# Gates of a decoder layer: six pairs of column chunks with seven products for eight, and another use of the weight buffers

## The chip, the core and the metric

The kernel runs on one core of a Trainium2 chip. The metric is the device time of one execution in microseconds (us). A core has TensorE (PE, matmuls; PEld is its weight load), VectorE (DVE), ScalarE (ACT), GpSimd (POOL) and SyncE (SP, which issues most of the DMAs). Each engine works off its own instructions in a fixed order; semaphores make one wait for another. Operands lie in SBUF, sums of matmuls in eight PSUM banks.

## What is computed

One layer on 256 tokens of width 2048, in float32. Its parts, cut from the reference:

```python
h = layer_norm(ALPHA * h + 0.5 * swiglu(h, w_ffn1_up, w_ffn1_down), ln1_g, ln1_b)
mix = token_mix(h, mem, w_in, b_gate, ...)
h = layer_norm(ALPHA * h + mix, ln2_g, ln2_b)
h = layer_norm(ALPHA * h + 0.5 * swiglu(h, w_ffn2_up, w_ffn2_down), ln3_g, ln3_b)

def token_mix(...):
    z = h @ w_in
    q, k, v, qi, ki, wi, u, qm, gl = split(z)
    a = dsa_attention(q, k, v, qi, ki, wi)      # 8 heads of 128, the 64 best keys of an indexer
    p = multiscale_pool(u, w_pool, pool_scale)
    m = memory_attention(qm, mem, w_mem_kv)     # 4 heads
    gates = sigmoid(gl + b_gate).reshape(B, S, 3, D)
    y = gates[0] * (a @ w_br_att) + gates[1] * (p @ w_br_pool) + gates[2] * (m @ w_br_mem)
    return y @ w_out
```

The gates are the part that the change touches: a product of the 256 x 2048 activations with 2048 x 6144 weights, 3 branches of 4 column chunks of 512.

## The kernel before

**Precision.** Every fp32 operand is split into a high and a low part (fp32r): ACT casts the high part (L105), DVE subtracts for the low one (L106). A product is three matmuls, high x high, high x low, low x high. Weights come by SP in halves of 128x1024 (two of the 128-row blocks of a group of 512 rows, `load_half`), into nine `raw` buffers; `halves` splits one into small buffers `wh` and `wl`, four of each, or, if `paged`, into two pages of the common pool `pg`.

**Work on PE.** `gemm` makes one 512-wide column chunk for both token halves (tt0, tt1, one PSUM bank each): 2 x 16 x 3 = 96 matmuls (L161) for a depth of 2048. With `head` or `tail` it holds some groups of weights back and runs tt0 over them, then tt1, so that one half begins or ends sooner; the line with `paged=` says which held halves lie in pages. `pair` makes two column chunks at once and saves one of eight quarter products in the first group of rows (seven products for eight, by sums of weights and sums of activations, `forms`): 186 matmuls (L231) for 192. Its sums of weights are DVE's (L256, L267, L272, L273). It consists of a front (one, two, five, six, seven), a middle and a back of whole quarters. `stream` weaves the front of the next pair with the back of the last, which is held in `self.back`; `flush` ends it. FFN1, FFN2 and their down products use pairs (20 for up, and some of the down products); the gates before do not.

**Delayed work.** `later` queues generators (the transposes of a chunk, `place`; the heads of an attention, `attend_heads`, six stages for four heads), and `tick` advances the first of them by one stage. A `gemm` ticks once per group of four blocks, `stream` once behind each middle step from the third on. One stage of `attend_heads` is the scores of one head (L445 on PE; L463, L465, L438, L440, L441 on DVE, the exponential L439 on ACT), the transposes of the head before (L477 and the split into `pt`) and the weighted sum of the one before that (L445 into `tr`, `weigh`). The order on each engine is set once, when the kernel is built, by the order of the program and by the scheduler's idea of what is ready.

**Order around the gates.** `attend(0)` makes q, k and v of heads 0 to 3 and queues their attention; gate(0) follows (three gemms, one for each branch), then `attend(1)`, gate(1), the rest of the queue, branch(0), gate(2), branch(1), gate(3), branch(2), branch(3). A gate adds its bias on DVE (L829) and takes tanh on ACT (L830). `branch` multiplies (L871) and adds the branches (L876, L877). Then come w_out with norm2 (`project_norm`), whose second token half is normalised inside FFN2's first gemm (`between=rest`), and FFN2 with norm3. In `Norm`, L554 (L552 for the first sum) adds the product to the residual, L556 and L605 take the statistics, L595 and L597 apply them in four pieces for each token half, and the last L597s write what goes out.

Of the kernel before, what the change touches and what calls it, by code (L numbers as in the profile page):

```python
# [17 lines left out]
P = 128  # L18
# [6 lines left out]
ND = D_MODEL // 512  # L25
# [9 lines left out]
TAKEN = -3e38  # L35
W_CHUNKS = dict(q=(0, 1), k=(2, 3), v=(4, 5), qi=(6, 7), u=(8,), qm=(9,))
GL0 = 10
PAGES = dict(pg=22, gt=6)
TMPS = 8
HIDDEN = ((0, 4), (4, 8), (8, NFF))  # L40

# [1 line left out]
class Layer:  # L43
# [19 lines left out]
    def hold(self, page):  # L63

        self.mark = self.nc.gpsimd.tensor_copy(self.tile("held", [P, 1], F32, 2), page.bitcast(F32)[:, :1])
# [18 lines left out]
        return self.sb.tile(shape, dt, name=f"{tag}_{self.n}", tag=tag, bufs=bufs)  # L84

    def page(self, dt=F32, tag="pg"):
        return self.tile(tag, [P, 1024], dt, PAGES[tag])

    def pages(self, n, dt=F32R, tags=()):
# [57 lines left out]
    def gemm(self, act, w, groups, head=0, tail=0, before=None, cut=None, between=None):  # L147

        nc = self.nc
        accs = [self.acc(), self.acc()]
        kts = 4 * groups
        self.products = []

        def step(tt, kt, wh, wl):
            ah, al = act(kt, tt)
            for i, (a, b) in enumerate(((ah, wh), (ah, wl), (al, wh))):  # L160
                self.products.append(nc.tensor.matmul(accs[tt], lhsT=a, rhs=b, start=kt == 0 and i == 0,  # L161
                                                      stop=kt == kts - 1 and i == 2))

        held = []
        for g in range(groups):
            if before is not None:
                before(g)
            ws = self.load_w(w[g], paged=g < head - 2 or groups - tail <= g < groups - 2,
                             cut=cut if g == 0 else None)
            parts = [(4 * g + kk, ws[kk // 2][0][:, kk % 2, :], ws[kk // 2][1][:, kk % 2, :]) for kk in range(4)]  # L170
            held += parts
            if g < head - 1 or groups > g + 1 > groups - tail:
                continue
            if g == head - 1 or g >= groups - tail:
                order = [(tt, part) for tt in range(2) for part in held]
            else:
                order = [(tt, part) for part in held for tt in range(2)]
            for i, (tt, part) in enumerate(order):
                if between is not None and g == head - 1 and i == len(held):
                    between()  # L180
                step(tt, *part)
            held = []
            self.tick()
        return accs
# [107 lines left out]
    def stream(self, parts):  # L292

        front, middle, back = parts
        behind = self.back
        for i in range(max(len(front), len(behind))):
            for step in behind[i:i + 1] + front[i:i + 1]:
                step()
        self.back = back
        for i, step in enumerate(middle):  # L300
            step()
            if i > 1:
                self.tick()
# [20 lines left out]
    @staticmethod  # L324
    def part(page, tt):
        return page.rearrange("p (k t) -> p k t", k=4)[:, :, tt * P:(tt + 1) * P]
# [86 lines left out]
    def project_norm(self, act, w, groups, resid, g, b, finish):  # L413

        norm = Norm(self, resid, g, b)
        norm.load()
        norm.load_scales()
        norm.add(act, w, groups, True, True, None, 4)
        return norm.finish(finish, defer=True)

    def norm_to_feature(self, dram):
# [196 lines left out]
def layer_kernel(ctx: ExitStack, tc: tile.TileContext, x, xT, memT, up1, down1, w_in, w_kw, b_gate, w_kv, w_pool,  # L618
                 pool_scale, br_att, br_pool, br_mem, w_out, up2, down2, ln, consts, band_c, out):
    nc = tc.nc  # L620
    L = Layer(ctx, tc)
# [70 lines left out]
    hh, hl = L.out_pages  # L692
    act = L.act_pages(hh, hl)
# [22 lines left out]
    for kt in range(KD):  # L716
        c = slice((kt % 8) * P, (kt % 8) * P + P)
# [14 lines left out]
    for i in range(2):  # L732
        r, c = slice(64 * i, 64 * i + 64), slice(256 * i, 256 * i + 256)
# [83 lines left out]

    gates = {}

    def gate(c):  # L820
        for br in range(3):
            n = br * ND + c
            accs = L.gemm(act, w_in[GL0 + n], 4)
            bg = L.tmp()
            nc.gpsimd.dma_start(bg, bass.AP(tensor=b_gate.tensor, offset=b_gate.offset + 512 * n, ap=[[0, P], [1, 512]]))
            gt = gates[br, c] = L.page(tag="gt")
            for tt in range(2):
                s = gt[:, 512 * tt:512 * tt + 512]
                nc.vector.tensor_add(s, accs[tt], bg)  # L829
                nc.scalar.activation(s, s, AF.Tanh, scale=0.5)  # L830

    ah, al = L.pages(2), L.pages(2)

# [13 lines left out]
    def attend(hf):  # L847
        q = feature_chunk(proj("q", hf), SCALE)
        k = feature_chunk(proj("k", hf))
        v = token_chunk(proj("v", hf))  # L850
        L.drain()
        if hf == 0:
            choose()
        L.later(L.attend_heads(4, *q, *k, *v, ah[hf], al[hf], 4 * hf, True, (dist, msel)))

    attend(0)
    gate(0)
    attend(1)
    gate(1)
    L.drain()  # L860
    yh, yl = [], []

    def branch(c):
        acts = ((L.act_pages(ah, al), br_att, 2), (L.act_pages([ph], [pl]), br_pool, 1),
                (L.act_pages([mh], [ml]), br_mem, 1))
        for br, (a, w, groups) in enumerate(acts):
            accs = L.gemm(a, w[c], groups)
            gt = gates[br, c]
            for tt in range(2):
                s = gt[:, 512 * tt:512 * tt + 512]  # L870
                nc.vector.scalar_tensor_tensor(s, s, 1.0, accs[tt], op0=ALU.add, op1=ALU.mult)  # L871
        yh.append(L.page(F32R))
        yl.append(L.page(F32R))
        for tt in range(2):
            g = [gates[br, c][:, 512 * tt:512 * tt + 512] for br in range(3)]
            nc.vector.tensor_add(g[0], g[0], g[1])  # L876
            nc.vector.tensor_add(g[0], g[0], g[2])  # L877

        def place():
            for tt in range(2):  # L880
                L.to_feature(gates[0, c][:, 512 * tt:512 * tt + 512], yh[c], yl[c], tt, 0.5)
            yield

        L.later(place())

    branch(0)
    gate(2)
    branch(1)
    gate(3)
    branch(2)  # L890
    branch(3)

# [78 lines left out]
```

## Time and profile before

| | |
|---|---|
| median of 3 runs | 2205.24 us (2204.08 to 2206.10) |
| profiled execution | 2204.89 us, its span 2203.0 us |
| granted TensorE clock, mean | 0.997 |
| busy: PE, DVE, ACT, POOL | 99%, 73%, 50%, 2% |
| chain that ended last | PE 97%, DVE 1%, DMA 1% |
| mean DMA rate | 201 GB/s |

Busy shares are means over the whole span; the rows by stage further on say which engine waits where. FFN1 fills the span up to about 700 us, the mixing block from there to about 1475 us, FFN2 the rest. A row `L106 DVE ... wl<-raw,wh` is a weight half's low part. The time in square brackets in a row of a timeline is the idle time of the engine before it, and what ended it.

### The profile page before, as it was taken

The page shows a single profiled execution, that of the slowest core. Times are in us where ns is not written, and L with a number is a line of the kernel's source. Part 1 is how long each engine was busy: PE and PEld are TensorE (multiplying, and loading weights), DVE is VectorE, ACT ScalarE, POOL GpSimd, SP SyncE. Part 2 cuts the span into 40 slices and gives each one's busy share as a digit, 9 for nine tenths or more (in the row PEclk, how much of TensorE's full clock was granted, in tenths as well). Part 3 has the DMA queues.
Part 4 walks back from the last instruction along what each step waited for, and adds up shares of the span by engine and source line. Part 5 has one row for each costly group of instructions (what it writes and reads, how often), then busy time and mean ns, then how long its engine had stood idle before and what let it go on. Part 6 is the DMA issues. An engine that isn't in the chain of part 4 may idle for free.

```text
span 2203.0 us, 26381 instructions
## 1 busy us (share of the span) xinstructions
PE 2181.2 (99%) x9886; PEld 1805.4 (82%) x9886; DVE 1607.1 (73%) x1819; ACT 1099.9 (50%) x1257; POOL 54.4 (2%) x98
## 2 busy tenths in 40 slices
PE   9999999999999999999999999999999999999997
PEld 7888888888888888888888888878888888888886
DVE  6878777887787858574566556677788677877786
ACT  5654555554554545544444444434555555545552
POOL 0000000000000100000000000000000000000000
PEclk9999999999999999999999999999999999999999
DMA  7575665565667645556655556754656655655762
GB/s 278 208 241 173 213 209 180 193 208 201 218 207 235 237 157 194 182 177 198 203 177 191 194 190 219 245 197 157 234 197 208 209 180 198 204 196 186 246 207 87
DMA packets 123136, 442.47 MB, mean 201 GB/s; under 512 B 14256, under 2 KB 14768, under 8 KB 123008
## 3 DMA queue, kind: packets, MB, share of 16 engines
q1 hardware_dynamic: 115632, 416.34, 55.1%
q0 software_dynamic: 6800, 22.36, 3.3%
q10 hardware_dynamic: 576, 2.10, 0.3%
q8 instruction: 77, 1.26, 0.2%
q14 instruction: 51, 0.42, 0.1%
HBM read 434.44 MB, written 6.29 MB: 200 GB/s over the span
## 4 chain that ended last, share of the span: by engine, by line
PE 97%; DVE 1%; DMA 1%; ACT 0%; issue 0%; POOLq 0%; POOL 0%; DVEq 0%; SPq 0%; ACTq 0%
PE acc L231 56%; PE acc L161 38%; PE tr L321 2%; PE tr L445 1%; DMA raw<-in_up 1%; DVE wl L106 0%; ACT wh L105 0%; PE tr L477 0%; DVE pg L106 0%; DVE gt L595 0%; DVE tmp L385 0%; DVE raw L267 0%; DVE gt L597 0%; PE tr L801 0%; DVE stats L556 0%
## 5 line engine op out<-in xcount | busy, mean ns | idle before, releaser
L106 DVE TENSOR_TENSOR wl<-raw,wh 128x1024 fp32r<-128x1024 f32 (+1 forms) x866 | 1054.2, 1220 | 532.7 <-ACT wh L105 522.7
L105 ACT CAST wh<-raw 128x1024 fp32r<-128x1024 f32 (+1 forms) x866 | 910.4, 1052 | 963.0 <-PE acc L231 444.4
L231 PE MATMUL acc<-wh,pg 128*128 128x512 f32 x3656 | 1137.6, 390 | 0.0
L231 PEld LDWEIGHTS acc<-wh,pg 128*128 128x128 f32 x3656 | 686.0, 188 | 142.4 <-DVE pg L106 0.6
L161 PE MATMUL acc<-wh,pg 128*128 128x512 f32 x2416 | 755.5, 390 | 1.2 <-ACT wh L105 1.0
L231 PE MATMUL acc<-wl,pg 128*128 128x512 f32 x1828 | 711.5, 389 | 0.3
L161 PEld LDWEIGHTS acc<-wh,pg 128*128 128x128 f32 x2416 | 453.8, 188 | 96.0 <-ACT wh L105 2.9
L161 PE MATMUL acc<-wl,pg 128*128 128x512 f32 x1208 | 470.7, 390 | 0.8 <-DVE wl L106 0.8
L231 PEld LDWEIGHTS acc<-wl,pg 128*128 128x128 f32 x1828 | 343.3, 188 | 71.1 <-DVE wl L106 1.1
L161 PEld LDWEIGHTS acc<-wl,pg 128*128 128x128 f32 x1208 | 227.0, 188 | 47.5 <-DVE wl L106 1.7
L362 ACT COPY tmp<-acc 128x512 f32<-128x512 f32 x80 | 47.1, 589 | 27.1 <-PE acc L231 27.1
L106 DVE TENSOR_TENSOR pg<-tr,pg 128x512 fp32r<-128x512 f32 x82 | 54.5, 683 | 0.4 <-ACT pg L105 0.3
L569 DVE TENSOR_TENSOR gt<-gt,acc 128x512 f32<-128x512 f32 x64 | 43.2, 681 | 6.0 <-PE acc L231 6.0
L105 ACT CAST pg<-tr 128x512 fp32r<-128x512 f32 x82 | 45.7, 589 | 0.0
L272 DVE TENSOR_TENSOR raw<-raw,raw 128x1024 f32<-128x1024 f32 x30 | 36.7, 1224 | 1.0
L267 DVE TENSOR_TENSOR raw<-raw,raw 128x1024 f32<-128x1024 f32 x30 | 36.7, 1224 | 1.0
L273 DVE TENSOR_TENSOR raw<-raw,raw 128x1024 f32<-128x1024 f32 x30 | 36.7, 1224 | 0.8
L256 DVE TENSOR_TENSOR raw<-raw,raw 128x1024 f32<-128x1024 f32 x30 | 36.7, 1224 | 0.8
L161 PE MATMUL acc<-pg,pg 128*128 128x512 f32 x120 | 30.7, 410 | 4.6 <-DVE pg L106 2.4
L321 PEld LDWEIGHTS tr<-ident,tmp 128*128 128x128 f32 x240 | 29.1, 140 | 6.5
L321 PE MATMUL tr<-ident,tmp 128*128 128x128 f32 x240 | 34.3, 272 | 0.0
L161 PEld LDWEIGHTS acc<-pg,pg 128*128 128x128 f32 x120 | 23.2, 197 | 11.0 <-DVE pg L106 3.7
(124 smaller groups left out, 672.6 us busy)
## 6 DMA issues: line engine op xcount, KB each, us to landing
raw<-in_up SPq DMA_DIRECT2D x350, 512.0 KB, 4.7
raw<-in_down SPq DMA_DIRECT2D x176, 512.0 KB, 4.5
raw<-in_w_in SPq DMA_DIRECT2D x176, 512.0 KB, 3.9
raw<-in_w_out SPq DMA_DIRECT2D x32, 512.0 KB, 4.7
raw<-in_w_kv SPq DMA_DIRECT2D x16, 512.0 KB, 4.9
raw<-in_br_att SPq DMA_DIRECT2D x16, 512.0 KB, 4.0
h_d<-gt POOLq DMA_DIRECT2D x16, 256.0 KB, 5.1
raw<-in_br_pool SPq DMA_DIRECT2D x8, 512.0 KB, 3.8
```

The source lines that it names most:

```text
L105: self.nc.scalar.copy(h, src)
L106: self.nc.vector.tensor_sub(l, src, h.bitcast(F32))
L161: self.products.append(nc.tensor.matmul(accs[tt], lhsT=a, rhs=b, start=kt == 0 and i == 0, stop=kt == kts - 1 and i == 2))
L231: nc.tensor.matmul(banks[bank], lhsT=a, rhs=b[:, k, :], start=fresh and k == 0 and i == 0, stop=(close is not None or left[bank] == 0) and ...
L256: nc.vector.tensor_add(raw["00"], raw["00"], raw["01"])
L267: nc.vector.tensor_add(raw["00"], raw["00"], raw["11"])
L272: nc.vector.tensor_add(raw["00"], raw["00"], raw["10"])
L273: nc.vector.tensor_add(raw["01"], raw["01"], raw["11"])
L321: self.nc.tensor.transpose(t[:, i * P:(i + 1) * P], src[:, i * P:(i + 1) * P], self.ident)
L362: nc.scalar.copy(s[name], bank)
L445: self.nc.tensor.matmul(out, lhsT=a, rhs=b, start=start and i == 0, stop=stop and i == 2)
L569: (nc.vector.tensor_sub if name in ("16", "167") else nc.vector.tensor_add)(zz, zz, bank)
```

## The change

The gates become six pairs: `gate(br, c, forms)` makes the chunks c and c+1 of one branch. gate(0,0) stands behind `attend(0)` and is flushed; gate(1,0) and gate(2,0) behind `attend(1)`; gate(0..2, 2) behind branch(0) and branch(1). The forms of the activations are made once, behind `attend(0)`. The sums of a pair (`take`) go to DVE, seven or eight of 128x512 for a pair. `stream` ticks behind each front step too. The two sets of pages (22 and 6) become one of 28. Of held groups the first two now use the small buffers and the later ones pages, and w_out's tail is 3 groups, no longer 4.

```diff
-PAGES = dict(pg=22, gt=6)
+PAGES = dict(pg=28)
...
     def page(self, dt=F32, tag="pg"):
+        tag = "pg"
         return self.tile(tag, [P, 1024], dt, PAGES[tag])
...
-            ws = self.load_w(w[g], paged=g < head - 2 or groups - tail <= g < groups - 2,
+            ws = self.load_w(w[g], paged=2 <= g < head or g >= groups - tail + 2 > 2,
                              cut=cut if g == 0 else None)
...
             for step in behind[i:i + 1] + front[i:i + 1]:
                 step()
+            self.tick()
...
-        norm.add(act, w, groups, True, True, None, 4)
+        norm.add(act, w, groups, True, True, None, 3)
...
-    def gate(c):
-        for br in range(3):
-            n = br * ND + c
-            accs = L.gemm(act, w_in[GL0 + n], 4)
-            bg = L.tmp()
-            nc.gpsimd.dma_start(bg, bass.AP(tensor=b_gate.tensor, offset=b_gate.offset + 512 * n, ap=[[0, P], [1, 512]]))
-            gt = gates[br, c] = L.page(tag="gt")
-            for tt in range(2):
-                s = gt[:, 512 * tt:512 * tt + 512]
-                nc.vector.tensor_add(s, accs[tt], bg)
+    def gate(br, c, forms):
+
+        bg = []
+        for n in (br * ND + c, br * ND + c + 1):
+            bg.append(L.tmp())
+            nc.gpsimd.dma_start(bg[-1], bass.AP(tensor=b_gate.tensor, offset=b_gate.offset + 512 * n,
+                                                ap=[[0, P], [1, 512]]))
+        gt = [L.page(tag="gt") for _ in range(2)]
+        for i in range(2):
+            gates[br, c + i] = gt[i]
+
+        def take(name, bank):
+            to = {"1": "00", "5": "01", "16": "01", "167": "11"}.get(name, name)
+            tt, i = int(to[0]), int(to[1])
+            s = gt[i][:, 512 * tt:512 * tt + 512]
+            if name in ("1", "5", "10"):
+                nc.vector.tensor_add(s, bank, bg[i])
+            elif name == "167":
+                nc.vector.tensor_sub(s, bg[i], bank)
+            elif name == "16":
+                nc.vector.tensor_sub(s, s, bank)
+            else:
+                nc.vector.tensor_add(s, s, bank)
+            if name == to:
                 nc.scalar.activation(s, s, AF.Tanh, scale=0.5)
+
+        w = [w_in[GL0 + br * ND + c + i] for i in range(2)]
+        L.stream(L.pair(act, forms, *w, 4, take, lambda: None))
...
     attend(0)
-    gate(0)
+    forms = L.forms(hh[0], hl[0])
+    gate(0, 0, forms)
+    L.flush()
     attend(1)
-    gate(1)
+    gate(1, 0, forms)
+    gate(2, 0, forms)
+    L.flush()
     L.drain()
...
     branch(0)
-    gate(2)
     branch(1)
-    gate(3)
+    for br in range(3):
+        gate(br, 2, forms)
+    L.flush()
     branch(2)
     branch(3)
```

In all the changed kernel has 36 matmuls less on PE, 72 instructions more on DVE and 19 more on ACT. Its line numbers are shifted by one or two from L106 on: L105 is L106, L106 is L107, L256 L257, L267 L268, L272 L273, L273 L274, L445 L447, L463 L465, L465 L467, L438 L440, L440 L442, L441 L443, L552 L554, L554 L556, L595 L597, L597 L599; the gate's bias add L829 becomes the takes L838 to L844, L871 L894, L876 L899, L877 L900, and L110 L111.

DVE in the first four heads' attention, before: one head's scores (L463 to L441) and the transposed head before (`pt`), with the next weight half `wl` behind them; two more halves and two bias adds stand between this and the next L463.

```order
L463 SCALAR_TENSOR_TENSOR s_1587_7878<-pg_6047,tr_7874 128x128
L463 SCALAR_TENSOR_TENSOR s_1590_7890<-pg_6047,tr_7886 128x256
L106 TENSOR_TENSOR pt_7869<-tr_7864,pt_7868 128x128
L465 TENSOR_TENSOR s_1587_7878<-s_1587_7878,pg_6134 128x128
L465 TENSOR_TENSOR s_1590_7890<-s_1590_7890,pg_6134 128x256
L438 TENSOR_REDUCE sm_7881<-s_1587_7878 128x1
L438 TENSOR_REDUCE sm_7893<-s_1590_7890 128x1
L440 RECIPROCAL sm_7881<-sm_7881 128x1
L441 TENSOR_SCALAR s_1587_7878<-s_1587_7878,sm_7881 128x128
L440 RECIPROCAL sm_7893<-sm_7893 128x1
L441 TENSOR_SCALAR s_1590_7890<-s_1590_7890,sm_7893 128x256
L106 TENSOR_TENSOR wl_8041<-raw_8038,wh_8040 128x1024
```

DVE at the same place of the changed kernel, inside the front of gate(0,0): the third head's last scaling (L443), and the fourth head's scores.

```order
L107 TENSOR_TENSOR wl_7953<-raw_7794,wh_7952 128x1024
L443 TENSOR_SCALAR s_1588_7830<-s_1588_7830,sm_7833 128x128
L443 TENSOR_SCALAR s_1591_7842<-s_1591_7842,sm_7845 128x256
L107 TENSOR_TENSOR pg_6983<-tr_7809,pg_6981 128x512
L840 TENSOR_TENSOR pg_7705<-tmp_7702,acc_7715 128x512
L107 TENSOR_TENSOR pt_7876<-tr_7871,pt_7875 128x256
L465 SCALAR_TENSOR_TENSOR s_1599_7885<-pg_6047,tr_7881 128x128
L465 SCALAR_TENSOR_TENSOR s_1602_7897<-pg_6047,tr_7893 128x256
L107 TENSOR_TENSOR pt_7876<-tr_7871,pt_7875 128x128
L467 TENSOR_TENSOR s_1599_7885<-s_1599_7885,pg_6134 128x128
L467 TENSOR_TENSOR s_1602_7897<-s_1602_7897,pg_6134 128x256
L440 TENSOR_REDUCE sm_7888<-s_1599_7885 128x1
```

The heads have moved together: no weight half stands between two heads' steps here, but one take and one split of the attention's output do.

DVE behind branch(1) in the changed kernel: the last products with the gates (L894), the branch sum (L900), and then the front of gate(0,2), with the scaled splits (L111) of the finished branch between.

```order
L894 SCALAR_TENSOR_TENSOR pg_9049<-pg_9049,acc_9768 128x512
L894 SCALAR_TENSOR_TENSOR pg_9049<-pg_9049,acc_9769 128x512
L900 TENSOR_TENSOR pg_7705<-pg_7705,pg_9049 128x512 x2
L838 TENSOR_TENSOR pg_9818<-acc_9829,tmp_9814 128x512
L107 TENSOR_TENSOR wl_9867<-raw_9820,wh_9866 128x1024
L111 SCALAR_TENSOR_TENSOR pg_9809<-tr_9837,pg_9808 128x4x128
L111 SCALAR_TENSOR_TENSOR pg_9809<-tr_9844,pg_9808 128x4x128
L268 TENSOR_TENSOR raw_9820<-raw_9820,raw_9864 128x1024
L838 TENSOR_TENSOR pg_9819<-acc_9871,tmp_9816 128x512
L107 TENSOR_TENSOR wl_9880<-raw_9820,wh_9879 128x1024
```

Before, weight halves of the next gemm stood at this place, each for 12 matmuls; now a half and a sum of weights stand behind each other for 6.

DVE at the end of the program, before: the last L597s of tt0, then the sum of tt1 (L554) and its statistics.

```order
L597 SCALAR_TENSOR_TENSOR gt_12983<-gt_12983,mv_17253,gt_16625 128x512
L597 SCALAR_TENSOR_TENSOR gt_12984<-gt_12984,mv_17253,gt_16626 128x512
L597 SCALAR_TENSOR_TENSOR gt_12985<-gt_12985,mv_17253,pg_16627 128x512
L597 SCALAR_TENSOR_TENSOR gt_12986<-gt_12986,mv_17253,pg_16628 128x512
L554 TENSOR_TENSOR gt_12986<-gt_12986,acc_17140 128x512
L556 BN_STATS stats_16649<-gt_12986 128x6
L605 BN_AGGR mv_17272<-stats_16649 128x2
```

DVE at the end of the changed kernel, the same instructions (now L599, L556, L558, L607).

```order
L556 TENSOR_TENSOR pg_13081<-pg_13081,acc_17235 128x512
L599 SCALAR_TENSOR_TENSOR pg_13078<-pg_13078,mv_17348,pg_16720 128x512
L599 SCALAR_TENSOR_TENSOR pg_13079<-pg_13079,mv_17348,pg_16721 128x512
L599 SCALAR_TENSOR_TENSOR pg_13080<-pg_13080,mv_17348,pg_16722 128x512
L599 SCALAR_TENSOR_TENSOR pg_13081<-pg_13081,mv_17348,pg_16723 128x512
L558 BN_STATS stats_16744<-pg_13081 128x6
L607 BN_AGGR mv_17367<-stats_16744 128x2
```

The sum of tt1 has moved ahead of tt0's four last steps, and its statistics behind them.

## Rows read from the trace of the kernel before

**Rows 1.** The page's first part: busy us, share of the span, instructions.
```profile
PE 2181.2 (99%) x9886; PEld 1805.4 (82%) x9886; DVE 1607.1 (73%) x1819; ACT 1099.9 (50%) x1257; POOL 54.4 (2%) x98
```

**Rows 2.** The page's fourth part: the chain that ended last, by engine.
```profile
PE 97%; DVE 1%; DMA 1%; ACT 0%; issue 0%; POOLq 0%; POOL 0%; DVEq 0%; SPq 0%; ACTq 0%
```

**Rows 3.** Busy time by stretch, last columns granted clock, DMA share, GB/s.
```profile
core 0: us, PE busy (x) PEld busy (x) DVE busy (x) ACT busy (x) POOL busy (x), PEclk, DMA share, GB/s
...
776.00:1060.00 284.00, 284.00 (x1362) 238.49 (x1362) 177.80 (x298) 138.97 (x201) 6.96 (x13) 1.00 0.55 183
1060.00:1200.00 140.00, 140.00 (x657) 117.13 (x656) 85.90 (x121) 64.60 (x88) 1.60 (x3) 1.00 0.56 188
1200.00:1470.00 270.00, 270.00 (x1207) 223.84 (x1206) 160.36 (x172) 111.76 (x116) 11.37 (x21) 1.00 0.60 206
...
```

**Rows 4.** Timeline of PE near the end: start, us, engine, line, tiles, count.
```profile
2186.21 0.39 PE L161 MATMUL acc<-wl,pg 128*128 128x512 f32 x1
...
2190.97 0.39 PE L161 MATMUL acc<-wl,pg 128*128 128x512 f32 x1
```

**Rows 5.** Timeline of DVE in the attention of heads 0 to 3.
```profile
978.02 1.28 DVE L829 TENSOR_TENSOR gt<-acc,tmp 128x512 f32<-128x512 f32 x2
979.22 1.21 DVE L106 TENSOR_TENSOR wl<-raw,wh 128x1024 fp32r<-128x1024 f32 x1
980.35 0.68 DVE L106 TENSOR_TENSOR pg<-tr,pg 128x512 fp32r<-128x512 f32 x1
980.95 0.41 DVE L106 TENSOR_TENSOR pt<-tr,pt 128x256 fp32r<-128x256 f32 x1
...
982.55 0.60 DVE L438 TENSOR_REDUCE sm<-s 128x1 f32<-128x128 f32 x2
983.45 0.16 DVE L440 RECIPROCAL sm<-sm 128x1 f32<-128x1 f32 x1 [0.30 <-ACT s L439]
...
984.14 0.35 DVE L441 TENSOR_SCALAR s<-s,sm 128x256 f32<-128x256 f32 x1
```

**Rows 6.** Timeline of PE at the seam from w_out to FFN2.
```profile
1469.51 1.91 PE L321 MATMUL tr<-ident,gt 128*128 128x128 f32 x16
1471.17 0.48 PE L161 MATMUL acc<-wl,pg 128*128 128x512 f32 x1
...
1473.54 0.39 PE L161 MATMUL acc<-wh,pg 128*128 128x512 f32 x1
1476.08 0.51 PE L161 MATMUL acc<-pg,pg 128*128 128x512 f32 x1 [2.15 <-ACT pg L105]
1477.34 5.99 PE L161 MATMUL acc<-pg,pg 128*128 128x512 f32 x18 [0.76 <-DVE pg L106]
1484.97 1.19 PE L161 MATMUL acc<-pg,pg 128*128 128x512 f32 x4 [1.64 <-DVE pg L106]
```

**Rows 7.** Groups of DVE, shapes apart: count, busy us, mean ns, idle before.
```profile
L272 DVE TENSOR_TENSOR raw<-raw,raw 128x1024 f32<-128x1024 f32 x30 | 36.7, 1224 | 1.0
...
L193 DVE TENSOR_TENSOR pg<-pg,pg 128x1024 f32<-128x1024 f32 x8 | 9.7, 1216 | 0.0
...
L197 DVE TENSOR_TENSOR pg<-pg 128x256 f32<-128x256 f32 x8 | 3.4, 422 | 0.1
```

**Rows 8.** Timeline of PE in the first pair's front of FFN1.
```profile
56.86 0.61 PE L231 MATMUL acc<-wh,pg 128*128 128x512 f32 x2
57.62 0.50 PE L231 MATMUL acc<-wl,pg 128*128 128x512 f32 x1
```

**Rows 9.** Timeline of DVE at the end, second token half.
```profile
2191.62 0.69 DVE L554 TENSOR_TENSOR gt<-gt,acc 128x512 f32<-128x512 f32 x1
...
2196.99 1.41 DVE L597 SCALAR_TENSOR_TENSOR gt<-gt,mv,gt 128x512 f32<-128x512 f32 x2
```

**Rows 10.** Busy time by stretch, behind the seam's waits (columns as in rows 3).
```profile
1478.40:1482.00 3.60, 3.60 (x10) 2.65 (x9) 3.25 (x6) 0.47 (x1) 0.86 (x1) 0.53 0.74 221
```

## Prediction, made blind

> **What bounds the kernel now.** I read the page's shares first. TensorE (PE) is busy for 99% of the span, VectorE (DVE) for 73% [rows 1], and 97% of the chain that ended last is PE [rows 2]. So a matmul taken away is worth its own time, as long as PE is still fed. The busy shares by stage say more: from 776 us, where the projections begin, to 1470 us, where w_out ends, PE has no idle time at all, while DVE is busy for 63%, 61% and 59% [rows 3]. All the gates lie in there. Three matmuls of 128x512 start every 0.68 us, seven times in the 4.76 us between the two rows shown: 0.227 us for one [rows 4]. A saved matmul is worth that; a wait of PE in this stage is lost in full, since no later wait of PE's is there to take it up.
>
> DVE is the second engine to watch. Each weight half costs it a subtraction of 1.21 us, 1.13 us from start to start [rows 5], and PE has 12 matmuls for a half (2.7 us) in an ordinary gemm, but only 6 (1.36 us) for a half in the front of a pair.
>
> **What the change removes.** Twelve gate gemms of 96 matmuls become six pairs of 186: 6 x 6 = 36 matmuls less, 36 x 0.227 = -8.2 us.
>
> **Window 1, gate(0,0), costs the most.** The pair brings DVE five sums and takes in its front, and the new tick behind each front step pulls all six stages of the first four attention heads into that front. Before, 24 gate matmuls stood between two such stages. The order of the changed kernel has, between the end of the v gemm on PE and the transposes of the fourth head, 44 gate matmuls and 51 small ones. A 128-wide transpose takes 0.104 us in a row of 16 [rows 6]; attention's pieces are 128 or 256 wide, so 0.104 to half of 0.227, and I take 0.11. PE's own work: 44 x 0.227 + 51 x 0.11 = 15.6 us.
>
> DVE has, in the same stretch and in this order, after the end of v: two splits of v, the four heads, the forms, six weight halves, one sum, four takes and one split of the attention's output. From the rows: a take or a split of 128x512 is 0.60 from start to start, a half 1.13 [rows 5]. One head runs from 980.95 to 984.49 us, 3.54 [rows 5]: 2.20 up to the end of the two L438, 0.30 of waiting for ScalarE's exponential, and 1.04 for four short pieces that are about 0.7 back to back. With other work in the gaps it is 2.9. The last two pieces of the last head (0.5 us) are not needed. Sum: 4 x 2.9 - 0.5 = 11.1; six halves 6.8; the 1.22 us sum [rows 7] 1.14; the forms, one of 1.22, four of 0.42 and one split [rows 7], 3.6; v 1.2; takes 2.4; output 0.6. That is 26.8 us, and it starts 0.6 us after v ends, behind ScalarE's cast: 27.4. If the exponential is waited for as in the trace, each head is 0.6 longer: 29.8. I take 28, near the first, since rows of the pair lie between the steps of a head. PE runs out: 28 - 15.6 = **12 us** of waiting (11.8 to 14.2). How far DVE can be ahead beforehand is limited: the four small buffers hold halves that PE has not used yet, and the splits of v cannot begin before v ends.
>
> **Window 2, gate(1,0)**, is the same with the other four heads: 51 gate matmuls and 51 small ones on PE, 51 x 0.227 + 51 x 0.11 = 17.2 us. DVE: heads 11.1, seven halves 7.9, one sum 1.14, takes 2.4, three splits 1.8, and the 0.6 at the start: 24.9, or 27.3 with the exponentials. Taken 25.2: **8 us** (7.7 to 10.1).
>
> **Window 3, gate(0,2).** It stands behind branch(1), whose last two products and sums, and a scaled split, are queued on DVE ahead of the front. From the end of branch(1) to the half that PE needs: nine of 128x512 at 0.60, six of 128x1024 at 1.13 to 1.14, 0.4 until the first begins: 12.6 us. PE has 33 matmuls and 8 transposes: 8.3. **4 us** (3 to 6). The other three gate pairs are woven with the back of the pair before, where PE has 12 matmuls more for each front step, as in FFN1 and FFN2; I cost them at nothing. Nor do the queues cost anything: the bias loads stay twelve, on POOL, and move ahead of the pair's matmuls; the weight loads on SP are as many as before, and the DMA engines are busy for 0.55 to 0.60 of the stage [rows 3]. One set of 28 pages in place of two adds no instruction.
>
> **FFN pairs.** The tick also moves the transposes of the last chunk up into the front. In the first pair of each FFN nothing is woven, and PE already waits there: two matmul starts are 0.76 apart around 57 us, where two pitches are 0.45, so 0.31 [rows 8]. Two splits of 0.60 now come ahead of halves there, eight transposes (0.83) give part of it back: +0.5 each, **+1** (0 to 2). The 20 woven pairs: 0, with an upper bound of the same 0.31 each, 6.
>
> **Seam from w_out to FFN2.** Small buffers first, and tail 3 for 4. Before, 20 matmuls started in the 11.43 us from 1473.54 to 1484.97, which is 6.9 us more than 20 pitches [rows 6]: three waits and the clock behind them, because FFN2's first halves stood on DVE behind the last sum of w_out. Now halves 1 to 4 come early or right behind that sum, but halves 5 and 6 stand behind the whole normalisation of the second token half (about 3.9 us, then 2.7): my sum of the waits is 0.6 + 0.9 + 0.4 + 3.5 + 2.4 = 7.8, against 6.9 before. **+1** (-5, if all but the first waits go, to +3).
>
> **Tail.** The last gemm's third group no longer has pages and must wait for small buffers, so the first token half ends 20 matmuls before the end instead of 36: 4.5 us instead of 8.2. Its four last steps (L597, 0.70 each, L599 in the changed file) then stand on DVE behind the sum of the second half. Before, the second half needed 5.37 us from its sum (L554) to its first last step [rows 9]. Now the first half's own 5.37 end 0.8 us after the second half's sum could begin; that sum and the four steps fill 3.4 us more; then comes the rest of the second half's chain, 5.37 less its sum's 0.7: 0.8 + 3.4 + 4.65 = 8.85, against 5.37: **+3.5** (2 to 4).
>
> **Clock.** After the waits at the seam the granted clock was 0.53 for 3.6 us, that is the 1.2 GHz level for nearly all of it, and ten matmuls started there instead of sixteen [rows 10]; so about 1.3 us lost. Behind windows 1 and 2 I put +1 each, **+2** (0 to 16, rival 2).
>
> The Trainium skill says, in "TensorE: Matmul & The Clock Gate", part 1 on the clock gate, that "the default state is throttled, and activity releases the throttle". It speaks against a change that thins PE out for 28 us to save 8; rival 2 is what that rule would make here. The seam row agrees with it; no row shows it for a stretch in which PE works half of the time.
>
> **Sum.** -8.2 + 12 + 8 + 4 + 1 + 1 + 3.5 + 2 = +23.3. Against the profiled execution (2203.0 span + 1.9 outside = 2204.9, 0.3 below the median) that is **2228 us**, 1.05% slower.
>
> **Rivals.**
> 1. *DVE keeps up* (the other side, not slower). If DVE's stretch in the windows is no longer than PE's, the waits of 12, 8 and 4 and the clock go: 2204.9 - 8.2 + 1 + 1 + 3.5 = 2202; and if the seam gets its 5 us back instead of losing one, 2196. It decides at 15.6 us of DVE work in window 1 and 17.2 in window 2. For it: DVE is idle for 40% of the mixing stage [rows 3], and at the FFN front PE waited only 0.31 [rows 8]. Against it: the sums are 1.5 times that, and are made of rows that stand in a fixed order. 0.12 for the first time, which is within the bound of no change; 0.14 for the second, since a DVE that keeps up in the windows would do so at the seam, where its queue is shorter.
> 2. *The clock falls inside the windows.* At 1.2 GHz PE's own work there is about twice 15.6 and 17.2, 31 and 34 us, now longer than DVE's 28 and 25: 3 + 9 more, and some 2 us at each end: 2226 + 12 + 4 = 2242. For it: the seam's 0.53 [rows 10]. Against it: in the windows PE waits in many short pieces, not one long one. 0.12.
> 3. *The pairs save, the waits are half* (the seam gains and the windows are at their lower ends or partly taken up): 2212 to 2216. 0.10.
>
> **How the numbers follow.** Forecast 2228, own range 2219 to 2238, with 0.52. About 0.2% (4.4 us) can be told from no change here. Faster by more: 0.14; within: 0.12; slower: 0.74. The range that should hold the time 8 times in 10 leaves out rival 1's faster part and the top of rival 2: 2203 to 2244.
>
> **What would show it.** Right: PE has idle pieces between 1000 and 1250 us that sum to about 20 us, released by DVE's splits of s, pt and weight halves, while DVE has none there; about 4 us idle behind branch(1); the last L599 of the second token half ends 3.5 us later behind the last matmul than before; the seam still shows 5 to 8 us of waits. Wrong: PE at full busy share through both attention windows, or DVE idle in them; then rival 1. A granted clock of 0.5 to 0.8 in the windows would be rival 2. The forecast rests most on the order of DVE in windows 1 and 2; if the waits there are short, nothing else carries it.

## The result, and the profile after

The changed kernel takes 2235.49 us (median of 4 runs, 2234.43 to 2237.53), the kernel before beside it 2204.66. The ratio is 1.014, 95% interval 1.0123 to 1.0158: 30.8 us slower. The profiled execution took 2234.8 us with a span of 2233.0, 30.0 more than before. First the page: its shares by engine, and by engine of the chain that ended last.

```profile
PE 2187.8 (98%) x9850; PEld 1803.4 (81%) x9850; DVE 1672.6 (75%) x1891; ACT 1125.4 (50%) x1276; POOL 52.8 (2%) x98
...
PE 94%; DVE 3%; issue 1%; ACT 1%; DMA 0%; SPq 0%; POOL 0%; POOLq 0%; DVEq 0%; ACTq 0%
```

PE has 36 matmuls less than in [rows 1] and is busy for longer; of the chain, 3% is DVE's, where [rows 2] had 1%. The same stretches in both kernels, the kernel before first (columns as in [rows 3]): the two attention windows, the stretch behind branch(1), the seam.

```profile
950.00:1000.00 50.00, 50.00 (x252) 42.43 (x251) 35.46 (x70) 25.64 (x46) 0.54 (x1) 1.00 0.50 173
1080.00:1125.00 45.00, 45.00 (x227) 38.17 (x227) 32.03 (x66) 23.35 (x42) 0.54 (x1) 1.00 0.55 182
1210.00:1250.00 40.00, 40.00 (x178) 33.13 (x177) 19.06 (x17) 17.11 (x18) 0.00 (x0) 1.00 0.55 191
1460.00:1520.00 60.00, 55.45 (x251) 45.01 (x250) 44.27 (x63) 23.42 (x28) 6.29 (x10) 0.97 0.52 171
```

And the changed kernel:

```profile
950.00:1000.00 50.00, 42.11 (x188) 33.61 (x187) 39.62 (x81) 24.19 (x44) 0.54 (x1) 0.90 0.38 130
1080.00:1125.00 45.00, 38.78 (x183) 30.84 (x183) 36.76 (x74) 22.75 (x42) 0.54 (x1) 0.96 0.39 135
1210.00:1250.00 40.00, 36.29 (x152) 28.52 (x151) 31.99 (x37) 16.95 (x19) 0.00 (x0) 0.91 0.40 138
1460.00:1520.00 60.00, 54.85 (x247) 43.61 (x246) 43.29 (x60) 23.33 (x27) 6.30 (x10) 0.97 0.61 204
```

In the three gate stretches PE now starts 64, 44 and 26 matmuls fewer, is idle for 8, 6 and 4 us, and the granted clock is below 1 in each. PE's timeline in window 1 shows where it waits.

```profile
955.66 0.39 PE L232 MATMUL acc<-wh,pg 128*128 128x512 f32 x1
961.16 0.77 PE L232 MATMUL acc<-wh,pg 128*128 128x512 f32 x1 [5.12 <-DVE sm L442]
...
973.11 0.50 PE L232 MATMUL acc<-wh,pg 128*128 128x512 f32 x1 [0.15 <-DVE pg L842]
...
976.17 0.39 PE L447 MATMUL tr<-pt,pg 128*128 128x256 f32 x1 [0.30 <-ACT pt L106]
...
979.55 0.50 PE L232 MATMUL acc<-wl,pg 128*128 128x512 f32 x1 [1.75 <-DVE wl L107]
...
981.82 0.41 PE L479 MATMUL tr<-ident,s 128*128 128x128 f32 x1
```

DVE in the same window. Between 953.47 and 980.75 us, where the last row shown ends, it is idle for 1.4 us: 1.09 ahead of a row shown, 0.16 ahead of one that is not, and slivers under 0.15.

```profile
953.47 1.28 DVE L107 TENSOR_TENSOR pg<-acc,pg 128x512 fp32r<-128x512 f32 x2
954.66 1.22 DVE L194 TENSOR_TENSOR pg<-pg,pg 128x1024 f32<-128x1024 f32 x1
...
958.06 1.22 DVE L107 TENSOR_TENSOR wl<-raw,wh 128x1024 fp32r<-128x1024 f32 x1
...
959.20 1.22 DVE L107 TENSOR_TENSOR pg<-pg,pg 128x1024 fp32r<-128x1024 f32 x1
...
960.33 0.69 DVE L838 TENSOR_TENSOR pg<-acc,tmp 128x512 f32<-128x512 f32 x1
960.93 0.15 DVE L442 RECIPROCAL sm<-sm 128x1 f32<-128x1 f32 x1
...
967.79 0.29 DVE L107 TENSOR_TENSOR pt<-tr,pt 128x128 fp32r<-128x128 f32 x1 [1.09 <-ACT pt L106]
...
979.54 1.21 DVE L107 TENSOR_TENSOR wl<-raw,wh 128x1024 fp32r<-128x1024 f32 x1
```

The one long wait of PE, 5.1 us, ends when DVE has worked off the splits of v, the forms (L194 to the split at 959.20), a weight half, the first head's first rows and the first take (L838). The releaser is named by the row that came last, a short L442; what the program makes PE wait for there is L838. The matmul at 961.16 is the first of step six, which adds to the bank that L838 reads, and in PE's order it stands ahead of step five.

To put a size on each stretch I add up, over all starts of matmuls in it, what lies between two starts beyond the pitch of the first (0.227 us for 512 columns, 0.115 for 256, 0.106 for a transpose). This lost time counts waits and a halved clock alike. Starts of 512-wide matmuls some 0.2 us too far apart in an unbroken row are counted as clock; matmuls of fewer columns are left out of that count. In us:

| stretch | before | changed | of it clock |
|---|---|---|---|
| window 1, gate(0,0), 950 to 1000 | 0.8 | 15.1 | 1.8 |
| window 2, gate(1,0), 1080 to 1125 | 0.7 | 11.7 | 0.95 |
| window 3, gate(0,2), 1215 to 1260 | 0.0 | 7.9 | 2.3 |
| first fronts of FFN1 and FFN2 | 1.2 | 2.9 | 0 |
| seam, 1460 to 1520 | 7.4 | 8.7 | 0.8 |
| last matmul's start to the last L597 (L599) | 8.5 | 11.8 | |

The differences are 14.3, 11.0, 7.9, 1.7, 1.3 and 3.3 us; with -8.2 for the matmuls the sum is +31.3, where the spans differ by 30.0. If the clock's share is counted over all matmuls that start while the granted clock is 0.50, each at most one pitch late, it is 3.7, 1.4 and 2.6 us in the three windows. All of this is read from one trace of each kernel.

### The profile page after: what moved, and what is told of

Its sections match the earlier page's. It is cut to its first block, busy times and chain, and to the rows that moved or that the text cites. A ratio compares the mean times of both kernels' runs of the same rounds, so it can differ in the third digit from the quotient of the medians.

```text
span 2233.0 us, 26438 instructions
## 1 busy us (share of the span) xinstructions
PE 2187.8 (98%) x9850; PEld 1803.4 (81%) x9850; DVE 1672.6 (75%) x1891; ACT 1125.4 (50%) x1276; POOL 52.8 (2%) x98
## 4 chain that ended last, share of the span: by engine, by line
PE 94%; DVE 3%; issue 1%; ACT 1%; DMA 0%; SPq 0%; POOL 0%; POOLq 0%; DVEq 0%; ACTq 0%
PE acc L232 66%; PE acc L162 25%; PE tr L323 1%; PE tr L447 1%; DVE wl L107 1%; ACT wh L106 0%; DVE pg L107 0%; DVE pg L599 0%; DMA raw<-in_up 0%; DVE pg L597 0%; PE tr L479 0%; ACT tmp L364 0%; DVE raw L268 0%; POOL mv L609 0%; ACT pg L106 0%
## 5 line engine op out<-in xcount | busy, mean ns | idle before, releaser
L107 DVE TENSOR_TENSOR wl<-raw,wh 128x1024 fp32r<-128x1024 f32 (+1 forms) x888 | 1082.3, 1220 | 497.4 <-ACT wh L106 485.2
L106 ACT CAST wh<-raw 128x1024 fp32r<-128x1024 f32 (+1 forms) x888 | 934.5, 1053 | 921.4 <-PE acc L232 534.8
L232 PE MATMUL acc<-wh,pg 128*128 128x512 f32 x4400 | 1378.0, 392 | 10.3 <-DVE sm L442 5.1
L106 ACT CAST pg<-tr 128x512 fp32r<-128x512 f32 x82 | 46.3, 590 | 34.3 <-PE tr L323 34.0
L107 DVE TENSOR_TENSOR pg<-tr,pg 128x512 fp32r<-128x512 f32 x82 | 54.4, 684 | 1.4 <-ACT pg L106 1.3
L274 DVE TENSOR_TENSOR raw<-raw,raw 128x1024 f32<-128x1024 f32 x36 | 44.1, 1224 | 6.0 <-DMA raw<-in_up 5.0
L571 DVE TENSOR_TENSOR pg<-pg,acc 128x512 f32<-128x512 f32 x64 | 43.3, 681 | 3.7 <-PE acc L232 3.7
L268 DVE TENSOR_TENSOR raw<-raw,raw 128x1024 f32<-128x1024 f32 x36 | 44.1, 1224 | 1.1
L257 DVE TENSOR_TENSOR raw<-raw,raw 128x1024 f32<-128x1024 f32 x36 | 44.1, 1224 | 1.1
L273 DVE TENSOR_TENSOR raw<-raw,raw 128x1024 f32<-128x1024 f32 x36 | 44.0, 1223 | 1.1
L447 PE MATMUL tr<-pg,pg 128*128 128x256 f32 (+2 forms) x168 | 28.3, 313 | 1.7 <-ACT pg L106 0.9
```

What stands on the lines that cost most here:

```text
L106: self.nc.scalar.copy(h, src)
L107: self.nc.vector.tensor_sub(l, src, h.bitcast(F32))
L232: nc.tensor.matmul(banks[bank], lhsT=a, rhs=b[:, k, :], start=fresh and k == 0 and i == 0, stop=(close is not None or left[bank] == 0) and ...
L257: nc.vector.tensor_add(raw["00"], raw["00"], raw["01"])
L268: nc.vector.tensor_add(raw["00"], raw["00"], raw["11"])
L273: nc.vector.tensor_add(raw["00"], raw["00"], raw["10"])
```

## The experiments

The chips differ a little, so each run is compared with runs of the kernel before on its own chip, whose medians were 2206.4 (runs 1 to 4), 2205.8 (5 to 8), 2205.1 (9, 10) and 2205.5 (11, 12). "Above before" is the difference to these; the changed kernel's own is 30.8, from a chip of its own. "Front tick" is the tick behind each front step, "new holding" the new rule for held groups together with w_out's tail of 3; an unwoven front is one that has no back of a pair before it to be woven with. What a window lost is read from one trace of each run.

**1. No front tick.**

```diff
                 step()
-            self.tick()
         self.back = back
```

> The changed kernel without the tick behind each front step, nothing else. Theory (the tick squeezes four heads of attention into an unwoven front, where DVE needs 27 us and PE 16): window 1 falls from 14 us of lost PE time to about 6, since the splits of v, the forms and the takes still stand ahead of the fifth step on DVE; window 2 from 11 to about 2; the two FFN starts give back 1.6. 2235.5 - 8 - 9 - 1.6 = about 2217. Rival (the takes and sums on DVE alone make the waits, the heads would be hidden anywhere): windows 1 and 2 keep most of their 25 us, about 2231.

2220.51, 14.1 above before: 16.7 of the 30.8 go. Window 1 lost 10.9 (expected 6), window 2 lost 3.7 (expected 2), window 3 lost 4.3, the FFN starts were back at 1.2, and the seam lost 10.3, 1.6 more than in the changed kernel. The tick makes most of window 2, but only 4 us of window 1. The 3.6 us less in window 3 were not expected; most of them are the clock, which was granted at 1.00 from 1210 to 1250 us here and at 0.91 in the changed kernel.

**2. Old holding.**

```diff
-            ws = self.load_w(w[g], paged=2 <= g < head or g >= groups - tail + 2 > 2,
+            ws = self.load_w(w[g], paged=g < head - 2 or groups - tail <= g < groups - 2,
...
-        norm.add(act, w, groups, True, True, None, 3)
+        norm.add(act, w, groups, True, True, None, 4)
```

> The changed kernel with the old rule for which held groups lie in pages, and a tail of 4 groups in w_out. Theory: the tail's 3.3 us and the seam's 1.5 come back: about 2230.7, the three windows as they are. Rival (the new rule helps the seam and the tail costs nothing): 2235 or later.

2231.86, 25.4 above before: 5.4 go, near the 4.8 expected, but only the tail's part is as the theory has it. The tail's 3.3 us came back. The seam's 1.5 did not: it lost 9.0, against 8.7 in the changed kernel. And window 3, which the edit does not touch, lost 1.5 less (6.4). DVE's timeline at the end: the first half's last steps stand ahead of the second half's sum again, and the last of them ends 8.54 us behind the start of the last matmul (2217.40), as before.

```profile
2215.06 2.74 DVE L599 SCALAR_TENSOR_TENSOR pg<-pg,mv,pg 128x512 f32<-128x512 f32 x4
2217.83 0.69 DVE L556 TENSOR_TENSOR pg<-pg,acc 128x512 f32<-128x512 f32 x1
...
2223.20 2.74 DVE L599 SCALAR_TENSOR_TENSOR pg<-pg,mv,pg 128x512 f32<-128x512 f32 x4
```

The changed kernel there has the order that the prediction read:

```profile
2219.09 0.68 DVE L556 TENSOR_TENSOR pg<-pg,acc 128x512 f32<-128x512 f32 x1
2219.69 2.73 DVE L599 SCALAR_TENSOR_TENSOR pg<-pg,mv,pg 128x512 f32<-128x512 f32 x4
2222.34 0.69 DVE L558 BATCH_NORM_STATS2 stats<-pg 128x6 f32<-128x512 f32 x1
...
2226.98 2.74 DVE L599 SCALAR_TENSOR_TENSOR pg<-pg,mv,pg 128x512 f32<-128x512 f32 x4
```

**3. Both edits together.**

> Both of the above. Theory: the two are apart in time and add up: about 2212, that is still some 7 us above the kernel before, of which window 3 (gate(0,2) behind branch(1)) is 7 and what is left of window 1 is 6, against 8.2 saved. Rival (the pairs' savings are not realised): over 2217.

2216.22, 9.8 above before: 21.0 of the 30.8 go, and 16.7 + 5.4 = 22.1, so they add up to within about 1 us. The 9.8 that stay are more than the expected 7, because window 1 keeps 11.1 us.

**4. The gates as gemms**, all else as changed (the gate function and the calls of before put back).

> The changed kernel with the gates as the twelve gemms of before, in their old order; the tick behind front steps, the 28 pages and the new rule for held groups stay. Theory: no window, no saving, but the FFN starts (1.6), the seam (1.5) and the tail (3.3): 2204.7 + 6.4 = about 2211. Rival (the woven FFN pairs lose with the tick too): 2211 + 20 x 0.2 = 2215. Rival (all of the loss is in the gates): 2205.

2214.28, 7.9 above before, 6.4 expected. No window loses (1.6, 0.6 and 0.0 us); what is there is the FFN starts (2.9), the seam (8.7) and the tail (last matmul's start to the end of the span 15.1 us, before 11.8). The woven FFN pairs lose as little as before (FFN1 from 62 to 685 us: 3.3 us in 2786 matmuls, before 3.2), so the rival of 20 x 0.2 falls. At the FFN start PE now waits for a copy on ScalarE, in this run and in the changed kernel (here PE's row of the changed kernel):

```profile
60.18 0.50 PE L232 MATMUL acc<-wh,pg 128*128 128x512 f32 x1 [0.92 <-ACT tmp L364]
```

**5. Forms early**, on top of run 3.

```diff
+    forms = L.forms(hh[0], hl[0])
     qm = feature_chunk(proj("qm"), SCALE)
...
     attend(0)
-    forms = L.forms(hh[0], hl[0])
     gate(0, 0, forms)
```

> The kernel of the third run (no front tick, old holding), with the forms of the activations made before the memory queries' projection instead of right ahead of gate(0,0). Theory (what is left of window 1 is the forms on DVE, behind which the low part of the forms and the take of the first step stand): window 1's 11 us fall to about 3, so 8 us under the third run, 1.7 above the kernel before. Rival (it is the takes on DVE, which hold a PSUM bank that the fourth step adds to): 1 to 2 us under the third run only.

2209.61, 3.8 above before (ratio 1.0017, interval 1.0007 to 1.0026): 6 us under run 3. Window 1 falls from 11.1 to 4.1, while window 2, from 1068 us on in this run, keeps its 3.8 (run 3: 3.7). What PE waited for in run 3 is ScalarE's cast of the forms, which waits for their last row on DVE (L201). First ScalarE, then PE of run 3:

```profile
959.40 1.05 ACT L106 CAST pg<-pg 128x1024 fp32r<-128x1024 f32 x1 [2.95 <-DVE pg L201]
```

```profile
960.50 0.80 PE L232 MATMUL acc<-wh,pg 128*128 128x512 f32 x1 [5.29 <-ACT pg L106]
```

And PE at this place in run 5:

```profile
960.82 0.50 PE L232 MATMUL acc<-wh,pg 128*128 128x512 f32 x1 [0.65 <-DVE pg L842]
```

**6. Takes copied by ScalarE**, on top of run 3.

```diff
         def take(name, bank):
...
+            if name in ("1", "5", "16", "167"):
+                t = L.tmp()
+                nc.scalar.copy(t, bank)
+                bank = t
```

> The kernel of the third run with the four early takes copied out of PSUM by ScalarE first, as FFN1 and FFN2 do, and added on DVE from the copy. Rival (the takes on DVE hold the bank): window 1 falls by 5 us or more and window 3 by 2. Theory (the forms): PE still waits for the low part of the forms, the row just ahead of the first take; 0 to 2 us under the third run.

2219.94, 14.1 above before, so 4.3 over run 3: a miss for both, and the rival falls. Window 1 lost 10.9, with the same 5.28 us wait for the forms' cast; windows 2 and 3 lost 4.1 and 7.3 (run 3: 3.7 and 5.6), the seam 9.0 (7.4). The seam's part has a cause of its own (last section), and of window 3's the granted clock has some: it was 0.91 from 1210 to 1250 us, against 0.96 in run 3. That ScalarE's casts came late by its extra copies is not shown.

**7. Forms early and takes by ScalarE.**

> Both: forms early and takes by ScalarE. Theory: window 1 to about 1.5 us, window 3 from 5.6 to about 4, since its branch sums stay ahead of the front on DVE: 10 us under the third run, level with the kernel before or 1 us under it.

2211.22, 5.4 above before. A miss: no better than run 5 without the copies. Window 1 lost 4.3, window 2 4.1, window 3 4.8.

**8. Both attentions' projections first**, then the pairs, on top of run 7.

```diff
     attend(0)
-    gate(0, 0, forms)
-    L.flush()
     attend(1)
+    gate(0, 0, forms)
     gate(1, 0, forms)
```

> The kernel with both, and the three gate pairs of chunks 0 and 1 woven in one row behind both attentions' projections, so that two pairs' fronts stand unwoven and not three; the first four heads run beside the gemms of q, k and v. Theory (an unwoven front costs, a woven one not): window 2's 3.7 us go too: 3 to 4 us under the run before it, some 4 us under the kernel before. Rival (the heads lose more beside the projections, whose splits are DVE's too): level with it or above.

2208.0, 2.2 above before, 3.2 under run 7: one unwoven front less is worth about what it was expected to be, from a higher level. The stretch of gate(0,0), now from 1030 to 1070 us, still lost 3.4.

**9. Four pairs behind gemms.** Front tick and new holding out, forms early, takes on DVE, and branch 0's gates as gemms (`gate1`, the old gate for one chunk).

```diff
     attend(0)
-    gate(0, 0, forms)
-    L.flush()
     attend(1)
+    gate1(0)
+    gate1(1)
     gate(1, 0, forms)
...
-    for br in range(3):
+    gate1(2)
+    gate1(3)
+    for br in (1, 2):
         gate(br, 2, forms)
```

> No front tick, old holding, forms early, takes on DVE; both attentions' projections first; then the gates of branch 0 as plain gemms, followed by pairs for branches 1 and 2, for chunks 0 and 1 and again for chunks 2 and 3. So 4 pairs are left (24 matmuls, 5.4 us saved), and each unwoven front stands behind a gemm, as at the start of each FFN, instead of behind the splits of v or the branch sums. Theory (what a front loses is DVE's work queued ahead of it, and behind a gemm DVE has little): 0.3 to 0.8 us for each of two fronts, 4 us under the kernel before. Rival (any unwoven front loses 3 to 5 us): 1 to 4 us above it.

2205.22, ratio to before 1.0003 (0.9994 to 1.0012): level, where 4 us less were expected. A front behind a gemm lost 1.8 us, not 0.3 to 0.8. That is 3.6 of the 5.4 us saved; another 0.7 went at the transposes of a head (1059.81 us), and the 1.1 that would be left is less than the measurement tells apart. PE's rows of the first front:

```profile
1082.59 0.50 PE L232 MATMUL acc<-wl,pg 128*128 128x512 f32 x1 [0.18 <-DVE wl L107]
1084.92 0.50 PE L232 MATMUL acc<-wh,pg 128*128 128x512 f32 x1 [0.42 <-DVE pg L842]
1086.06 0.50 PE L232 MATMUL acc<-wl,pg 128*128 128x512 f32 x1 [0.64 <-DVE wl L107]
```

**10. The same four pairs in the old order** (gate1(0), gate1(1) between the two attentions).

> The same four pairs, with the gemm gates of branch 0 between the two attentions as before, so that the second four heads run in the middle steps of the pair gate(1,0), whose front stands behind the splits of v. Theory: window 2's 3 to 4 us stay: about level with the kernel before, 3 us above the run with both attentions first.

2205.3, level with run 9 and with before. The expected 3 us between the two orders are not there: the front behind the splits of v loses 0.8 us and the heads in the middle some 1, against 1.8 behind a gemm.

**11. Run 9 with takes by ScalarE.**

> The ninth run's kernel with the four early takes copied by ScalarE first. In the ninth each of the two fronts behind a gemm still lost 1.8 us, 0.9 of it at a half that stands behind a take on DVE, while the first front of each FFN, whose takes are ScalarE's copies, loses 0.3. Theory (takes on DVE inside the front): 0.3 to 1 us for each, 2 us under the ninth run, 1 to 2 us under the kernel before. Rival (the two bias adds of the gemm ahead of the front, which stay, or ScalarE's copies, which delay its casts as in the sixth run): level with the ninth or above.

2204.31, 1.2 under before; ratio 0.9995 (0.9987 to 1.0004), which is not told from no change. The fronts lost 1.1 us each, most of it now at a copy of ScalarE:

```profile
1084.99 0.50 PE L232 MATMUL acc<-wh,pg 128*128 128x512 f32 x1 [0.66 <-ACT tmp L839]
```

**12. The changed kernel, forms early, nothing else.**

> The changed kernel with front ticks, new holding and all, and only the forms made earlier, before the memory queries' projection. Theory now (DVE's row of work ahead of the front adds up, whoever brings it; the fourth step waits behind the forms): of window 1's 15 us the 5.3 us in one piece go, the heads' many short waits stay: about 5 to 7 us under the changed kernel. Rival (PE is held by the heads anyway, so the forms' place only moves the wait): 0 to 2 us under it. Window 2 is the comparison, since it has the heads but no forms: there 11 us were lost.

2230.95, 25.4 above before: 5.4 go. Window 1 fell from 15.1 to 10.0; window 2, with heads and no forms, lost 10.2, so the two are now alike. Windows 2 and 3, which the edit leaves as they were, lost 1.5 and 1.9 less than in the changed kernel, the seam 1.8 more: so much do two traces differ, by the granted clock. In window 2 it did not fall at all here (in the changed kernel 0.96):

```profile
1080.00:1125.00 45.00, 39.05 (x190) 30.67 (x189) 38.17 (x76) 23.79 (x44) 0.54 (x1) 1.00 0.43 142
```

In window 1 taking the tick away alone gives 4.2 us, moving the forms alone 5.1, and both 11.0 (runs 1, 12 and 5). The 1.7 us that both together give beyond the two alone are about the size of this scatter, and the times add up: 16.7 without the tick, 5.4 with the old holding and 5.4 with the forms early make 27.5, where run 5, with all three, is 27.0 under the changed kernel. Two causes that hide in each other are not shown.

## Why the prediction was right, point by point

2228 was forecast with a range of 2203 to 2244; 2235.5 came. The direction and the mechanism held: 36 matmuls less, and more than that lost where DVE's row in a front is longer than PE's. The forecast's terms add up to +23.3, the found ones to +31.3; windows 2 and 3 and the clock are where it was short, and no term was far too high, so the total does not rest on errors that cancel.

- **Savings, 8.2.** The matmuls are gone; no run measures them by themselves. The sum of the changed kernel's trace leaves room for them: over the whole span its starts lose 66.2 us where 30.8 were lost before, the tail takes 3.3 more, and less 8.2 that is 30.5, where the spans differ by 30.0.
- **Window 1, 12 forecast, 14.3 found**, of which 1.8 is clock that had its own term; without it 12.5 (10.6 if the clock is counted over all matmuls). The row of DVE that was summed to 26.8 takes 27.3 us on the trace, from 953.47 to the end of the sixth half at 980.75, of which it works 25.9. From the end of v (952.45) to the fourth head's transposes (981.82) PE needed 29.4 us, 28 forecast. What the sum does not tell is which row to take away: the heads that the tick pulls in are its largest term, 11.1 of 26.8, but without the tick 10.9 of 15.1 us stayed (run 1), while moving the forms, 3.6 in the sum, took 5.1 to 7.0 us (runs 12 and 5), because ScalarE's cast of them and steps five and six wait behind them.
- **Window 2, 8 forecast, 11.0 found**, 10.1 without the clock, at the top of the range given. The fourth head's transposes came 27.9 us behind the end of v (1082.99 to 1110.86), 25.2 forecast; the upper sum, with each exponential waited for, was 27.3. That it comes near is luck: DVE waits for no exponential here. From 1083.6 us to the transposes it works 25.0 us, as summed (24.9), and what the sum lacked is 2.1 us in which DVE waits within the heads, for ScalarE's cast of a transposed head (1.5 us) and for the scores on PE (0.6 us). From the changed kernel's waits of DVE, 1083 to 1111 us (us in total, times, longest):

```profile
DVE pt L107 <- ACT pt L106: 1.5, 3, 1.0
...
DVE s L465 <- PE tr L447: 0.6, 2, 0.5
```

PE's row at the start of the window and near its end:

```profile
1088.94 0.50 PE L232 MATMUL acc<-wl,pg 128*128 128x512 f32 x1 [2.12 <-DVE wl L107]
...
1103.38 0.50 PE L232 MATMUL acc<-wl,pg 128*128 128x512 f32 x1 [1.44 <-DVE wl L107]
...
1109.02 0.50 PE L232 MATMUL acc<-wh,pg 128*128 128x512 f32 x1 [0.72 <-ACT wh L106]
```

- **Window 3, 4 forecast, 7.9 found**, of which 2.3 is clock; the rest, 5.6, is in the range of 3 to 6. In run 1, with no fall of the clock there, the window lost 4.3. PE waits for the branch sum ahead of its transposes, for the cast of a half and its low part, and for a take, as the row was read:

```profile
1231.26 1.17 PE L323 MATMUL tr<-ident,pg 128*128 128x128 f32 x8 [0.58 <-DVE pg L900]
...
1236.97 0.50 PE L232 MATMUL acc<-wh,pg 128*128 128x512 f32 x1 [1.78 <-ACT wh L106]
1238.23 0.50 PE L232 MATMUL acc<-wl,pg 128*128 128x512 f32 x1 [0.76 <-DVE wl L107]
...
1241.10 0.80 PE L232 MATMUL acc<-wh,pg 128*128 128x512 f32 x1 [0.59 <-DVE pg L842]
```

- **FFN starts, +1 forecast, +1.7 found** (runs 1 and 4); the woven pairs cost nothing, as taken.
- **Seam, +1 forecast, +1.3 found.** The size agrees partly by luck: the seam lost 8.7 to 10.5 in the four traces with the new holding and 7.4 or 9.0 in those with the old one. PE's waits are where the sum had them, ahead of the end of w_out and at the halves that stand behind the normalisation. Rows of the changed kernel that answer to [rows 6]:

```profile
1495.87 1.32 PE L323 MATMUL tr<-ident,pg 128*128 128x128 f32 x8 [0.45 <-DVE pg L599]
1501.98 0.50 PE L162 MATMUL acc<-wl,pg 128*128 128x512 f32 x1 [0.89 <-DVE wl L107]
1509.61 2.93 PE L162 MATMUL acc<-pg,pg 128*128 128x512 f32 x6 [2.87 <-DVE pg L107]
1513.40 2.81 PE L162 MATMUL acc<-pg,pg 128*128 128x512 f32 x11 [0.86 <-DVE pg L107]
```

- **Tail, +3.5 forecast, +3.3 found**, and run 2 takes it away.
- **Clock, +2 forecast, about 5 found** in the three windows (7.7 if counted over all matmuls): the mis-sized term beside window 2. Window 3 had been given none, and has the largest part by the narrower count. Rows of the changed kernel by stretch:

```profile
956.00:961.00 5.00, 0.05 (x1) 0.00 (x0) 5.00 (x12) 2.49 (x4) 0.00 (x0) 0.86 0.00 0
961.00:966.00 5.00, 4.84 (x16) 3.93 (x17) 5.00 (x15) 1.37 (x5) 0.00 (x0) 0.50 0.28 104
980.00:983.00 3.00, 3.00 (x11) 2.28 (x10) 1.21 (x3) 0.00 (x0) 0.00 (x0) 0.52 0.67 223
1240.00:1243.00 3.00, 2.41 (x7) 1.52 (x6) 3.00 (x4) 0.74 (x1) 0.00 (x0) 0.50 0.78 273
```

A granted clock of 0.50 is the 1.2 GHz level. It comes with the 5.1 us wait and follows the 1.75 us wait and the waits of window 3; in window 1 part of it falls where PE would have waited for DVE anyway. Such waits do not always bring it: window 2 of run 12 lost 10.2 us at a granted clock of 1.00. Rival 2, the clock at that level through the whole windows, did not come: over window 1 it is 0.90, over window 2 0.96. The rule quoted from the Trainium skill ("TensorE: Matmul & The Clock Gate", part 1), by which activity releases the throttle, agrees with the changed kernel's rows. What the lowered clock cost here is the 5 to 8 us of 30 above.

Of the signs named ahead of the result, PE's idle time was put at about 20 us between 1000 and 1250 us. It is 9.9 there, since window 1 lies ahead of 1000 us; from 950 on it is 17.8 us. The tail's sign, 3.5 us, came as 3.3.

Rival 1 (DVE keeps up) falls in windows 1 to 3. It is what run 4 shows for gates as gemms and, nearly, what runs 9 to 11 show for four pairs.

## What to carry to other kernels

Before work is woven into the stretch of one engine, sum the row of each other engine between two points that the first must pass, with start-to-start times from the trace: 26.8 against 15.6 us said here, before any run, that an engine with 40% idle time in the stage would hold the other up. The sum tells that a wait comes, not which of its rows to move: taking away the heads, the largest term, was worth no more in window 1 than moving the forms, a third of it in the sum. A size that is read from one trace each moves by 1.5 to 2 us here with the granted clock, so compare a window with one that the edit does not touch before a small difference is explained. The matmuls saved (8.2 us of 2205) pay only if an unwoven front loses less than the pairs woven behind it save: six pairs with three such fronts may lose 2.7 us at each, and four pairs with two as much. The best version here, four pairs behind gemms, came out 1.2 us under the kernel before, within the measurement.

## What was not expected of the hardware

With the old holding the seam lost 7.4 us in most traces, 9.0 in runs 2 and 6, and its last wait has two sizes in kernels whose code there is the same: 1.80 us start to start beyond the pitch in runs 3, 5 and 9, 3.05 in runs 2 and 6. The granted clock is what differs. Before the change and in runs 3, 5 and 9 it fell ahead of this wait: 18 matmuls took 5.99 us, the clock was 0.53, and the wait behind them was 1.64 us [rows 6, rows 10]. In run 2 the same 18 took 4.74 us, the wait was 2.89 us, and the clock fell behind it:

```profile
1501.06 4.74 PE L162 MATMUL acc<-pg,pg 128*128 128x512 f32 x18 [0.76 <-DVE pg L107]
1508.69 1.63 PE L162 MATMUL acc<-pg,pg 128*128 128x512 f32 x5 [2.89 <-DVE pg L107]
```

```profile
1508.80:1513.00 4.20, 4.20 (x12) 3.37 (x13) 3.62 (x5) 0.00 (x0) 2.21 (x4) 0.61 0.72 261
```

The matmuls are 1.25 us longer and the wait 1.25 us shorter: DVE sets when the wait ends, so a slow stretch ahead of it costs nothing, and the same stretch behind it some 1.6 us. This is 1.6 of the 4.3 us of run 6. Why the clock falls now ahead of the wait and now behind it stays open.
